# A hybrid attention layer on one core: how stacks, values and bias tables come in from DRAM

## The chip, the core and the metric

The kernel runs on one core of one Trainium2 chip. The core has a matrix engine (TensorE, PE in the profile, with PEld for its weight loads), three engines for elementwise work (VectorE: DVE, ScalarE: ACT, GpSimd: POOL), a fifth engine that mostly issues transfers (SyncE: SP), and 16 DMA engines that move data between DRAM and the on-chip memory SBUF. SBUF has 128 partitions; matmul results land in a smaller memory, PSUM. Each engine works through its own list of instructions in order. The metric is the device time of one execution in microseconds (us): the median of several executions.

## The reference, cut to what matters

One encoder layer over 1024 tokens (a grid of 16 rows of 64) of width 1024, all in float32: a half-step feed-forward block (FFN1), a mixing block with 16 attention heads of width 64, and a second half-step feed-forward block (FFN2).

```python
x = x + 0.5 * rmsnorm(swiglu(rmsnorm(x, g0), w_gate, w_up, w_down), g1)      # FFN1
q, k, v = split(rmsnorm(x, g2) @ w_qkv)                                      # 16 heads each
o_na  = neighbourhood_attention(q[:, :8], k[:, :8], v[:, :8], rel_bias)      # heads 0..7
o_dil = dilated_mixture_attention(q[:, 8:], k[:, 8:], v[:, 8:], t5_bias)     # heads 8..15
x = x + rmsnorm(concat(rmsnorm(o_na, ga), rmsnorm(o_dil, gb)) @ w_out, g3)
x = x + 0.5 * rmsnorm(swiglu(rmsnorm(x, g4), w_gate2, w_up2, w_down2), g5)   # FFN2
```

In neighbourhood attention a query at (row, column) of the grid sees 8 rows by 16 columns of keys around it, with a learned bias by row and column distance. The dilated mixture computes, for every head, sliding windows over each token's neighbours with dilations 1, 4 and 16 (window 128, 512, 2048), with a bias by distance, and merges the three by their softmax denominators.

## The kernel before, in words

**Stages.** FFN1 comes first; the first matmul of the values starts at 683.7 us, the first scores at 941.0, and the last scores at 1194.6 ; pieces of the output projection run between the last heads, and the rest of it and FFN2 follow. The large matrix products use seven block products in place of eight, each as three matmuls of float32 operands split into a rounded upper part and the remainder (`hi`, `lo`).

**q and k.** The projection makes q and k of two heads (a pair p, 128 columns) at a time, in the order of `QK_ORDER`: pairs 4 to 7 (dilated) first, then 0 to 3 (neighbourhood). `QKPairs.put` splits each into upper part and remainder, which lie in the tile `e` of [128 partitions, 2, 512 tokens], and POOL writes them to a DRAM tile `c.qk[p][kind]` of shape [2, 128, 1024]: upper parts first, then remainders. In three cases the tokens are reordered on the way: q of the neighbourhood pairs (`strip`) comes by strips of 8 grid columns, k of the dilated pairs by token number modulo 4.

**Stacks.** A head's scores take two accumulating matmuls over 128 partitions: the 64 rows of q's upper part above the 64 rows of its remainder, against k's upper part (written into both halves), then against k's remainder (both halves). So `load_stack` fills a tile `st` of [128, 3, 1024]: slot 0 is q (upper part in partitions 0 to 63, remainder in 64 to 127), slots 1 and 2 are k's upper part and remainder, the same in both halves. It issues four transfers on POOL, two for each half of 64 partitions.

**Heads.** Attention goes through 16 heads, the eight dilated ones first (heads 0 to 7 in what follows) and the eight neighbourhood ones behind them (8 to 15). Each head is cut into units, and `Ctx.unit` runs them as a pipeline: scores on PE, bias and row maximum on DVE (`maxes`), exponentials on ACT (`exps`), transposes on PE (`turn`), copies back on ACT or DVE (`copy`), the product with the values on PE (`outs`). A dilated head has two parts of four units: `part` 1 for the dilations 4 and 16 with values `vb`, `part` 0 for dilation 1 with values `va`. For part 1, POOL first makes a copy `q` of slot 0 sorted by token number modulo 4 (`q_by_residue`). A neighbourhood head has eight units, one for each strip. Its bias table is `nb`, of which POOL adds the column mask `cmask` into a second half.

**What is loaded ahead.** `load_head` asks for a head's stack (POOL queue), for the values if the head is the first of its pair (SP queue), and then for its bias table (SP queue). `next_head` keeps one or two heads asked for ahead. In the dilated part, every third head's stack and bias table go to a pool of their own (`c.op`), so there are three stack buffers; in the neighbourhood part there are two (`c.stk`), so the stack of head n+2 waits until the scores of head n are done.

**Values in DRAM.** All values of a group of heads lie in `c.v[g]`, [1024 tokens, 4 pairs x 130], in the order of the tokens (a head has 64 columns and one of ones). `vrows` and `vearly` write them on POOL, 128 tokens at a time. `dil_values` reads them for the windows of dilation 1 (`va`: 11 blocks of 128 keys, each block sorted by token number modulo 4) in 12 transfers over 32 partitions, and for dilation 4 (`vb`) in 4 over 128; it is called twice, for the first pair and then for the other three together. `na_v` reads a pair's values by strips, `vs`, in 16 transfers of 8 partitions each.

**Order.** PE, DVE and ACT run in the order in which the program is written (`manual_schedule`). POOL and SP instructions are placed by a scheduler, by what each waits for; on the chip each of these two works through its list in order, so an instruction that waits holds up those behind it, the issuing of transfers included.

Of the kernel before, what the change touches and what calls it, by code (L numbers as in the profile page):

```python
# [19 lines left out]
P, T = 128, 512  # L20
# [776 lines left out]
class QKPairs:  # L797
# [19 lines left out]
    def put(self, b, kind, h, x):  # L817
# [18 lines left out]
        d = c.qk[p][kind]  # L836
        for j in range(2):
            if strip:
                dst = d[j].rearrange("p (s r c) -> p s (r c)", s=8, r=16)[:, :, h * 64:h * 64 + 64]
                nc.gpsimd.dma_start(dst, e[:, j].bitcast(F32).rearrange("p (s x) -> p s x", s=8))  # L840
            elif kind and p >= NP:
                dst = d[j].rearrange("p (c h t) -> p h c t", c=4, h=2)[:, h]
                nc.gpsimd.dma_start(dst, parts[j].bitcast(F32))
            else:
                nc.gpsimd.dma_start(d[j, :, h * T:(h + 1) * T], e[:, j].bitcast(F32))


def load_stack(c, p, hd, pool):

    nc = c.nc  # L850
    st = pool.tile([P, 3, SEQ], F32R, tag="st", name="st", bufs=2 if pool is c.stk else 1)
    rows = slice(hd * 64, hd * 64 + 64)
    q, k = c.qk[p]
    for u in range(2):
        dst = slice(u * 64, u * 64 + 64)
        nc.gpsimd.dma_start(st[dst, 0, :], q[u, rows, :])
        nc.gpsimd.dma_start(st[dst, 1:3, :], k[:, rows, :].rearrange("j p n -> p j n"))
    return st
# [41 lines left out]
def dil_values(c, pool, p, n):  # L900

    w, row = n * VW, 16 * VW
    va = pool.tile([P, 11, w], F32, tag="va", name="va", bufs=1)
    vb = pool.tile([P, 4, 2, w], F32, tag="vb", name="vb", bufs=1)
    v = c.v[1][:, (p - NP) * VW:(p - NP) * VW + w]
    for ci in range(4):
        to = va[ci * 32:ci * 32 + 32]
        for u0, m, t0 in ((0, 7, 16), (7, 2, 0), (9, 2, 192)):
            c.nc.sync.dma_start(to[:, u0:u0 + m], bass.AP(tensor=v.tensor, offset=v.offset + ci * 4 * VW + t0 * row,
                                                          ap=[[row, 32], [32 * row, m], [1, w]]))  # L910
    for ci in range(4):
        c.nc.sync.dma_start(vb[:, ci], v.rearrange("(j i c) f -> c i j f", j=2, c=4)[ci])
    return va, vb


class DilPair:
# [17 lines left out]

    def bias(self, hd, third):
        c, nc = self.c, self.c.nc
        g = (c.op if third else c.gp).tile([P, 3, 384], F32, tag="g", name="g", bufs=1 if third else 2)
        for i in range(2):
            nc.sync.dma_start(g[:, 2 - i], c.gab[i][2 * self.pi + hd, :, 127:511])
        return g  # L940
# [10 lines left out]
    def unit(self, hd, st, q, g, part, quad, un, po):  # L951
# [5 lines left out]
        def scores():  # L957
# [4 lines left out]
            for j in range(2):  # L962
# [8 lines left out]
                else:  # L971
# [5 lines left out]
                    ex = sj.rearrange("p (c u t) -> p u c t", c=4, u=2)  # L977
                    pj = pb[:, j].rearrange("p (u c t) -> p u c t", u=2, c=4)
# [79 lines left out]
def na_v(c, p):  # L1058
    vs = c.vp.tile([P, 8, VW], F32, tag="v" + "ab"[p % 2], name="vs")
    src = c.v[0][:, p * VW:(p + 1) * VW].rearrange("(r s c) f -> r c s f", r=16, s=8)  # L1060
    for r in range(16):
        c.nc.sync.dma_start(vs[r * 8:r * 8 + 8], src[r])
    return vs

# [106 lines left out]
def layer(tc, a, out):  # L1171
    nc = tc.nc
    c = Ctx(tc)
    with ExitStack() as ctx:
# [20 lines left out]
        c.qk = [[c.dr.tile([2, P, SEQ], F32, name=f"qk{p}_{k}") for k in range(2)] for p in range(8)]  # L1195
# [138 lines left out]
        def load_head():  # L1334
# [4 lines left out]
            st = load_stack(c, p, hd, c.op if third else c.stk)  # L1339
            if hd == 0:  # L1340
                pairs[p] = DilPair(c, p, attended if p == 2 * NP - 1 else lambda: None) if p >= NP else na_v(c, p)
            loaded.append((pairs[p], st, pairs[p].bias(hd, third) if p >= NP else na_bias(c, p, hd)))
# [15 lines left out]
        with ExitStack() as order:  # L1358
# [64 lines left out]
            def vearly(p, t, ps):  # L1423
# [3 lines left out]
                nc.gpsimd.dma_start(vs1[t] if p == 0 else c.v[0][t * P:(t + 1) * P, :], v)  # L1427
# [18 lines left out]
            def vrows(t, h):  # L1446
                for g in range(t < 4, 2):
                    nc.gpsimd.dma_start(c.v[g][t * P:(t + 1) * P, :], h[:, g])
# [227 lines left out]
```

## Time and profile before

| | |
|---|---|
| median of 3 runs | 1955.64 us (1953.23 to 1959.21) |
| profiled execution: its own time | 1954.08 us |
| its span, first to last instruction | 1952.3 us |
| PE busy | 1867.3 us (96%) |
| DVE, ACT, POOL busy | 1313.9 us (67%), 804.1 us (41%), 325.4 us (17%) |
| mean granted PE clock | 0.980 |
| moved by DMA | 400.97 MB, mean 205 GB/s |
| attention stage | 941 to 1197 us of the span, from the first scores to the end of the last head |

The profiled execution is one of its own; all busy times, waits and durations below come from it, and its own time is compared with its span and with the median of the runs. PE is counted busy from a matmul's start to its modelled end. The granted clock tells at what share of full speed the throttle let PE run in a stretch. A row of a timeline gives the start in us from the start of the span, the duration, the engine, the line of the kernel, the operation and its tiles (out<-in), how many like it follow one another, and in square brackets how long the engine stood idle before it and what ended that. A row of the table of stretches gives, for a window of time, each engine's busy time and instructions, the granted clock, the mean busy share of the 16 DMA engines (1.00 is all of them; it can read a little more), and the rate. POOL's transfers go by the queue q0, SP's by q1.

### The profile page before, as it was taken

How to read it: one execution, taken by the hardware profiler on the slowest of the kernel's cores; microseconds unless marked ns; L12 is line 12 of the kernel's file. 1: busy time of each engine (PE TensorE's matmuls, PEld its weight loads, DVE VectorE, ACT ScalarE, POOL GpSimd, SP SyncE). 2: the span in 40 equal slices, each digit the busy share in tenths (PEclk: the TensorE clock that was granted, in tenths of full speed). 3: DMA queues.
4: the chain of work that ended last, by engine and by line, in shares of the span. 5: the costliest groups of instructions: out<-in, count | busy, mean ns of one | idle time of the engine just before them, and what ended most of it. 6: DMA issues, size and time to landing. Idle time of an engine off the chain costs nothing.

```text
span 1952.3 us, 25216 instructions
## 1 busy us (share of the span) xinstructions
PE 1867.3 (96%) x9044; PEld 1559.5 (80%) x9044; DVE 1313.9 (67%) x2205; ACT 804.1 (41%) x1287; POOL 325.4 (17%) x536
## 2 busy tenths in 40 slices
PE   5999999999999989999899889998999999999997
PEld 4788888888888868778799887776888888888886
DVE  5778776765656766567456556676788777754557
ACT  4522333333534445233567655454222333344332
POOL 2101111111000123233443310121011111110000
PEclk8999999999999999999899989998999999999999
DMA  6555565546976667768997961574556665476663
GB/s 241 214 172 178 178 236 194 211 161 237 324 250 207 244 216 251 242 217 228 281 205 135 199 125 44 183 276 160 168 183 208 233 216 194 153 265 225 197 231 131
DMA packets 165246, 400.97 MB, mean 205 GB/s; under 512 B 18737, under 2 KB 35297, under 8 KB 165121
## 3 DMA queue, kind: packets, MB, share of 16 engines
q1 hardware_dynamic: 113616, 224.63, 36.4%
q0 software_dynamic: 50640, 172.64, 27.8%
q10 hardware_dynamic: 864, 2.10, 0.3%
q8 instruction: 71, 1.16, 0.2%
q14 instruction: 55, 0.44, 0.1%
HBM read 274.84 MB, written 129.50 MB: 207 GB/s over the span
## 4 chain that ended last, share of the span: by engine, by line
PE 78%; DMA 9%; DVE 6%; issue 5%; ACT 1%; POOL 1%; SPq 0%; DVEq 0%; POOLq 0%; ACTq 0%
PE mmp L264 16%; PE mmp L262 16%; PE mmp L263 16%; PE accp L263 7%; PE accp L264 7%; PE accp L262 7%; PE po L993 2%; PE ptp L892 2%; PE trp L170 1%; PE sp L981 1%; DMA vs<-v 1%; PE po L1106 1%; DMA g<-gab 1%; DMA x<-x 1%; DMA va<-v 1%
## 5 line engine op out<-in xcount | busy, mean ns | idle before, releaser
L262 PE MATMUL mmp<-x,whi 128*128 128x512 f32 (+1 forms) x1464 | 579.7, 396 | 7.6 <-ACT whi L355 3.6
L264 PE MATMUL mmp<-x,wlo 128*128 128x512 f32 (+1 forms) x1464 | 574.9, 393 | 1.0 <-DVE wlo L356 1.0
L263 PE MATMUL mmp<-x,whi 128*128 128x512 f32 (+1 forms) x1464 | 574.5, 392 | 0.6 <-DVE x L172 0.5
L262 PEld LDWEIGHTS mmp<-x,whi 128*128 128x128 f32 x1464 | 277.9, 190 | 67.5 <-ACT whi L355 4.2
L264 PEld LDWEIGHTS mmp<-x,wlo 128*128 128x128 f32 x1464 | 277.8, 190 | 62.2 <-DVE wlo L356 1.9
L263 PEld LDWEIGHTS mmp<-x,whi 128*128 128x128 f32 x1464 | 278.1, 190 | 59.8 <-DVE x L172 1.5
L613 DVE TENSOR_TENSOR pw<-praw,pw 128x1024 fp32r<-128x1024 f32 (+1 forms) x182 | 199.3, 1138 | 122.8 <-ACT pw L612 122.4
L612 ACT CAST pw<-praw 128x1024 fp32r<-128x1024 f32 (+1 forms) x182 | 169.5, 983 | 206.0 <-PE accp L264 167.7
L355 ACT CAST whi<-wraw 128x1024 fp32r<-128x1024 f32 x129 | 135.2, 1050 | 249.4 <-PE mmp L263 216.7
L262 PE MATMUL accp<-pw 128*128 128x512 f32 x600 | 234.4, 391 | 0.6 <-DVE hb L684 0.6
L264 PE MATMUL accp<-pw 128*128 128x512 f32 x600 | 233.5, 389 | 0.0
L263 PE MATMUL accp<-pw 128*128 128x512 f32 x600 | 233.4, 389 | 0.0
L356 DVE TENSOR_TENSOR wlo<-wraw,whi 128x1024 fp32r<-128x1024 f32 x129 | 157.6, 1225 | 24.9 <-ACT whi L355 24.8
L262 PEld LDWEIGHTS accp<-pw 128*128 128x128 f32 x600 | 112.6, 188 | 24.2 <-issue 1.0
L264 PEld LDWEIGHTS accp<-pw 128*128 128x128 f32 x600 | 112.6, 188 | 23.5
L263 PEld LDWEIGHTS accp<-pw 128*128 128x128 f32 x600 | 112.7, 188 | 23.3
L560 POOL DMA_DIRECT2D g<-sg x44 | 23.9, 542 | 472.3 <-DVE sg L553 285.6
L374 ACT COPY s<-mmp 128x512 f32<-128x512 f32 x52 | 30.5, 587 | 147.9 <-PE mmp L264 146.3
L518 DVE TENSOR_TENSOR c<-mmp,u 128x512 f32<-128x512 f32 x52 | 35.9, 691 | 82.5 <-PE mmp L264 82.2
L172 DVE TENSOR_TENSOR x<-trp,x 128x512 fp32r<-128x512 f32 x84 | 57.2, 687 | 35.0 <-ACT x L171 35.0
L355 ACT CAST whi<-traw 128x512 fp32r<-128x512 f32 x52 | 32.3, 621 | 116.9 <-PE mmp L263 58.4
L443 DVE TENSOR_TENSOR wraw<-wraw 128x1024 f32<-128x1024 f32 x52 | 63.6, 1224 | 23.6 <-DMA wraw<-in_wqk_dram 12.5
(230 smaller groups left out, 2739.2 us busy)
## 6 DMA issues: line engine op xcount, KB each, us to landing
praw<-g SPq DMA_DIRECT2D x70, 512.0 KB
wraw<-in_wg_dram SPq DMA_DIRECT2D x44, 512.0 KB
wraw<-in_wu_dram SPq DMA_DIRECT2D x44, 512.0 KB
tr<-in_wd_dram SPq DMA_DIRECT2D x44, 512.0 KB
g<-sg POOLq DMA_DIRECT2D x88, 256.0 KB, 3.9
ts<-tr POOLq DMA_DIRECT2D x22, 1024.0 KB, 4.7
praw<-ts SPq DMA_DIRECT2D x88, 256.0 KB
praw<-in_wd_dram SPq DMA_DIRECT2D x66, 256.0 KB
```

What stands on the lines that cost most here:

```text
L172: nc.vector.tensor_sub(lo, ps, hi.bitcast(F32))
L262: nc.tensor.matmul(out, ahi, bhi, start=start, stop=False, skip_group_check=go_on)
L263: nc.tensor.matmul(out, ahi, blo, start=False, stop=False, skip_group_check=go_on)
L264: nc.tensor.matmul(out, alo, bhi, start=False, stop=stop, skip_group_check=go_on)
L355: nc.scalar.copy(hi, raw)
L356: nc.vector.tensor_sub(lo, raw, hi.bitcast(F32))
L443: nc.vector.tensor_sub(r[:, 0:2], r[:, 1:3], r[:, 0:2])
L518: nc.vector.tensor_add(c21, d, u2)
L612: nc.scalar.copy(w[side][:, 0, :m], raw[:, :m])
L613: nc.vector.tensor_sub(w[side][:, 1, :m], raw[:, :m], w[side][:, 0, :m].bitcast(F32))
L892: c.nc.tensor.transpose(self.tps[:, j, :], self.probs[:, j * P:(j + 1) * P], c.ident)
L993: nc.tensor.matmul(po[0][:, un * 2 + j], u.pt[:, 2 * j + t, :], rhs, start=t == 0, stop=t == 1)
```

## The change: layouts in DRAM, and the order of asking

Four things are changed; the arithmetic stays as it is.

1. **Stacks.** `c.qk` has the shape [128, 2, 1024]: a row's upper part and remainder lie behind each other. `load_stack` issues two transfers of 128 partitions where there were four of 64. Their source patterns are written out as lists of [step, count], outermost first: for q [1024, 2], [2048, 64], [1, 1024]; for k [0, 2], [2048, 64], [1, 2048], where the step of 0 reads the same 64 rows twice. The writes of `put` that don't reorder tokens (48 before) become one transfer each instead of two.
2. **Values in the order of their use.** Rows of `c.v[0]` are ordered by strip, grid row and column in the strip, and those of `c.v[1]` in blocks of 64 tokens by the token number modulo 4. `put_values` writes 128 tokens as two transfers of 64 partitions, where there was one. `dil_values` has 3 transfers over 128 partitions for `va` in place of 12 over 32, and 8 of one block for `vb` in place of 4 of two blocks; `na_v` has 1 in place of 16.
3. **Bias ahead of values.** `load_head` asks for a head's bias table before a pair's values (`DilPair.bias` becomes the function `dil_bias`).
4. **Exponentials of part 0.** Since `va` now holds each block of 128 keys as two half blocks sorted by token number modulo 4, the exponentials read and write in groups of 16 (`m c i`) where they did so in groups of 32 (`u c t`). Their number and size stay.

```diff
@@ QKPairs.put
         d = c.qk[p][kind]
+        if not strip and not (kind and p >= NP):
+            nc.gpsimd.dma_start(d[:, :, h * T:(h + 1) * T], e.bitcast(F32))
+            return
         for j in range(2):
             if strip:
-                dst = d[j].rearrange("p (s r c) -> p s (r c)", s=8, r=16)[:, :, h * 64:h * 64 + 64]
+                dst = d[:, j].rearrange("p (s r c) -> p s (r c)", s=8, r=16)[:, :, h * 64:h * 64 + 64]
...
-            else:
-                nc.gpsimd.dma_start(d[j, :, h * T:(h + 1) * T], e[:, j].bitcast(F32))
@@ load_stack
     st = pool.tile([P, 3, SEQ], F32R, tag="st", name="st", bufs=2 if pool is c.stk else 1)
-    rows = slice(hd * 64, hd * 64 + 64)
-    q, k = c.qk[p]
-    for u in range(2):
-        dst = slice(u * 64, u * 64 + 64)
-        nc.gpsimd.dma_start(st[dst, 0, :], q[u, rows, :])
-        nc.gpsimd.dma_start(st[dst, 1:3, :], k[:, rows, :].rearrange("j p n -> p j n"))
+    q, k = [bass.AP(tensor=x.tensor, offset=x.offset + hd * 64 * 2 * SEQ, ap=[[step, 2], [2 * SEQ, 64], [1, n]])
+            for x, step, n in zip(c.qk[p], (SEQ, 0), (SEQ, 2 * SEQ))]
+    nc.gpsimd.dma_start(st[:, 0, :], q)
+    nc.gpsimd.dma_start(st[:, 1:3, :].rearrange("p j n -> p (j n)"), k)
     return st
@@ dil_values
-    w, row = n * VW, 16 * VW
+    w, row = n * VW, 64 * 4 * VW
...
-    for ci in range(4):
-        to = va[ci * 32:ci * 32 + 32]
-        for u0, m, t0 in ((0, 7, 16), (7, 2, 0), (9, 2, 192)):
-            c.nc.sync.dma_start(to[:, u0:u0 + m], bass.AP(tensor=v.tensor, offset=v.offset + ci * 4 * VW + t0 * row,
-                                                          ap=[[row, 32], [32 * row, m], [1, w]]))
-    for ci in range(4):
-        c.nc.sync.dma_start(vb[:, ci], v.rearrange("(j i c) f -> c i j f", j=2, c=4)[ci])
+    v, at = c.v[1], c.v[1].offset + (p - NP) * VW
+    for u0, m, m0 in ((0, 7, 1), (7, 2, 0), (9, 2, 12)):
+        c.nc.sync.dma_start(va[:, u0:u0 + m], bass.AP(tensor=v.tensor, offset=at + m0 * row,
+                                                      ap=[[4 * VW, P], [2 * row, m], [1, w]]))
+    for ci in range(4):
+        for j in range(2):
+            c.nc.sync.dma_start(vb[:, ci, j], bass.AP(tensor=v.tensor, offset=at + 8 * j * row + ci * 16 * 4 * VW,
+                                                      ap=[[row, 8], [4 * VW, 16], [1, w]]))
     return va, vb
+
+
+def dil_bias(c, pi, hd, third):
+    g = (c.op if third else c.gp).tile([P, 3, 384], F32, tag="g", name="g", bufs=1 if third else 2)
+    for i in range(2):
+        c.nc.sync.dma_start(g[:, 2 - i], c.gab[i][2 * pi + hd, :, 127:511])
+    return g
@@ DilPair.unit
-                    ex = sj.rearrange("p (c u t) -> p u c t", c=4, u=2)
-                    pj = pb[:, j].rearrange("p (u c t) -> p u c t", u=2, c=4)
+                    ex = sj.rearrange("p (c m i) -> p m c i", c=4, m=4)
+                    pj = pb[:, j].rearrange("p (m c i) -> p m c i", m=4, c=4)
@@ na_v
-    src = c.v[0][:, p * VW:(p + 1) * VW].rearrange("(r s c) f -> r c s f", r=16, s=8)
-    for r in range(16):
-        c.nc.sync.dma_start(vs[r * 8:r * 8 + 8], src[r])
+    c.nc.sync.dma_start(vs, c.v[0][:, p * VW:(p + 1) * VW].rearrange("(s p) f -> p s f", s=8))
     return vs
+
+
+def put_values(c, g, t, x):
+
+    for i in range(2):
+        if g:
+            dst = c.v[1].rearrange("(m c i) f -> m i c f", c=4, i=16)[2 * t + i]
+        else:
+            dst = c.v[0].rearrange("(s r c) f -> r s c f", s=8, r=16)[2 * t + i]
+        c.nc.gpsimd.dma_start(dst, x[i * 64:i * 64 + 64])
@@ the DRAM tiles
-        c.qk = [[c.dr.tile([2, P, SEQ], F32, name=f"qk{p}_{k}") for k in range(2)] for p in range(8)]
+        c.qk = [[c.dr.tile([P, 2, SEQ], F32, name=f"qk{p}_{k}") for k in range(2)] for p in range(8)]
@@ load_head
             st = load_stack(c, p, hd, c.op if third else c.stk)
+            g = dil_bias(c, p - NP, hd, third) if p >= NP else na_bias(c, p, hd)
             if hd == 0:
                 pairs[p] = DilPair(c, p, attended if p == 2 * NP - 1 else lambda: None) if p >= NP else na_v(c, p)
-            loaded.append((pairs[p], st, pairs[p].bias(hd, third) if p >= NP else na_bias(c, p, hd)))
+            loaded.append((pairs[p], st, g))
```

In `vearly` and `vrows`, where a write to `c.v[g]` stood, `put_values` is called.

The scheduler's order of SP changes where the first dilated heads are asked for, at the end of the q and k projections. `va` and `vb` are the two value tiles of dilated pairs (those ending in 130 of the first pair, in 390 of the three others), `g` is a head's bias table, `v1` and `gab` are their DRAM tiles; "x2" means two alike in a row. Before:

```order
L909 DMA va_7186<-v1_88 32x2x130 x2
L912 DMA vb_7187<-v1_88 128x2x130 x4
L939 DMA g_7204<-gab0_68 128x384
L939 DMA g_7204<-gab1_69 128x384
L939 DMA g_7414<-gab0_68 128x384
L939 DMA g_7414<-gab1_69 128x384
L909 DMA va_7493<-v1_88 32x7x390
L909 DMA va_7493<-v1_88 32x2x390 x2
```

And now, the same place of SP:

```order
L918 DMA g_7189<-gab0_68 128x384
L918 DMA g_7189<-gab1_69 128x384
L906 DMA va_7192<-v1_88 128x7x130
L906 DMA va_7192<-v1_88 128x2x130 x2
L910 DMA vb_7193<-v1_88 128x1x130 x8
L918 DMA g_7406<-gab0_68 128x384
L918 DMA g_7406<-gab1_69 128x384
L918 DMA g_7482<-gab0_68 128x384
L918 DMA g_7482<-gab1_69 128x384
L906 DMA va_7485<-v1_88 128x7x390
L906 DMA va_7485<-v1_88 128x2x390 x2
```

The bias of head 0 stands ahead of the first pair's values, and the bias tables of head 1 and of head 2 (the first of the second pair) ahead of the values of the three other pairs.

On POOL, among the neighbourhood heads, `st` is a stack, `qk` its two DRAM tiles (`_0` for q, `_1` for k), and the TENSOR_TENSOR adds the column mask into a bias table. Before:

```order
L1537 TENSOR_TENSOR nb_9072<-nb_9072,cmask_7481 128x384
L856 DMA st_9230<-qk1_0_73 64x1024
L857 DMA st_9230<-qk1_1_74 64x2x1024
L856 DMA st_9230<-qk1_0_73 64x1024
L857 DMA st_9230<-qk1_1_74 64x2x1024
L1537 TENSOR_TENSOR nb_9252<-nb_9252,cmask_7481 128x384
```

And now:

```order
L1548 TENSOR_TENSOR nb_9027<-nb_9027,cmask_7472 128x384
L855 DMA st_9185<-qk1_0_73 128x1x1024
L856 DMA st_9185<-qk1_1_74 128x1x2048
L1548 TENSOR_TENSOR nb_9188<-nb_9188,cmask_7472 128x384
L855 DMA st_9331<-qk1_0_73 128x1x1024
L856 DMA st_9331<-qk1_1_74 128x1x2048
```

A stack's two transfers stand where its four stood, each of 128 rows. The orders of PE, DVE and ACT are the same before and now, apart from line numbers.

More of the change, by code (lines that the diff above doesn't have):

```diff
@@ L836, in put @@
         d = c.qk[p][kind]
+        if not strip and not (kind and p >= NP):
+            nc.gpsimd.dma_start(d[:, :, h * T:(h + 1) * T], e.bitcast(F32))
+            return
         for j in range(2):
             if strip:
-                dst = d[j].rearrange("p (s r c) -> p s (r c)", s=8, r=16)[:, :, h * 64:h * 64 + 64]
+                dst = d[:, j].rearrange("p (s r c) -> p s (r c)", s=8, r=16)[:, :, h * 64:h * 64 + 64]
                 nc.gpsimd.dma_start(dst, e[:, j].bitcast(F32).rearrange("p (s x) -> p s x", s=8))
-            elif kind and p >= NP:
-                dst = d[j].rearrange("p (c h t) -> p h c t", c=4, h=2)[:, h]
+            else:
+                dst = d[:, j].rearrange("p (c h t) -> p h c t", c=4, h=2)[:, h]
                 nc.gpsimd.dma_start(dst, parts[j].bitcast(F32))
-            else:
-                nc.gpsimd.dma_start(d[j, :, h * T:(h + 1) * T], e[:, j].bitcast(F32))
 def load_stack(c, p, hd, pool):
@@ L933, in outputs @@
         self.ob = c.op.tile([P, 8, RW], F32, tag="ob", name="ob")
[L935 to L940, printed above, removed]
     def head(self, hd, st, q, g, late, parts=(1, 0)):
@@ L1059, in na_v @@
     vs = c.vp.tile([P, 8, VW], F32, tag="v" + "ab"[p % 2], name="vs")
[L1060 to L1063 removed]
+    c.nc.sync.dma_start(vs, c.v[0][:, p * VW:(p + 1) * VW].rearrange("(s p) f -> p s f", s=8))
+    return vs
+def put_values(c, g, t, x):
+    for i in range(2):
+        if g:
+            dst = c.v[1].rearrange("(m c i) f -> m i c f", c=4, i=16)[2 * t + i]
+        else:
+            dst = c.v[0].rearrange("(s r c) f -> r s c f", s=8, r=16)[2 * t + i]
+        c.nc.gpsimd.dma_start(dst, x[i * 64:i * 64 + 64])
 def na_bias(c, p, hd):
@@ L1426, in vearly @@
                 nc.scalar.copy(by_head(v), ps.rearrange("p (h f) -> p h f", f=64))
-                nc.gpsimd.dma_start(vs1[t] if p == 0 else c.v[0][t * P:(t + 1) * P, :], v)
+                if p == 0:
+                    nc.gpsimd.dma_start(vs1[t], v)
+                else:
+                    put_values(c, 0, t, v)
             vp = Passes(c, 4, op, getv, vearly)
@@ L1447, in vrows @@
                 for g in range(t < 4, 2):
-                    nc.gpsimd.dma_start(c.v[g][t * P:(t + 1) * P, :], h[:, g])
+                    put_values(c, g, t, h[:, g])
             vp.take = combine(c, lambda t, g, h: None, vrows, True)
```

1 line of the change is left out of this document (removed).

## The prediction, as it was made before the run

> **What bounds the kernel now.** I read the page first (span, busy shares), then a table of stretches over the attention stage, then the timelines of PE and POOL there, and last the transfers from issue to landing.
>
> ```profile
> span 1952.3 us, 25216 instructions
> PE 1867.3 (96%) x9044; PEld 1559.5 (80%) x9044; DVE 1313.9 (67%) x2205; ACT 804.1 (41%) x1287; POOL 325.4 (17%) x536
> ...
> core 0: us, PE busy (x) PEld busy (x) DVE busy (x) ACT busy (x) POOL busy (x), PEclk, DMA share, GB/s
> 980.00:997.00 17.00, 12.88 (x92) 12.65 (x90) 7.92 (x35) 8.72 (x20) 7.66 (x8) 0.80 1.04 218
> 997.00:1070.00 73.00, 72.64 (x644) 72.40 (x642) 49.11 (x208) 54.06 (x124) 27.75 (x30) 1.00 0.79 153
> 1070.00:1114.00 44.00, 42.49 (x346) 40.93 (x344) 29.98 (x116) 31.28 (x70) 19.83 (x25) 1.00 1.12 199
> 1114.00:1143.00 29.00, 18.14 (x87) 16.81 (x86) 11.68 (x29) 11.37 (x26) 4.72 (x7) 0.59 0.64 117
> ```
>
> PE is busy for 96% of the span, so a change in transfers can only matter where PE stands still. Everything the change touches is used in the attention stage (941 to 1197 us). Dilated heads 0 to 7 run until 1070; from 997 to 1070 PE is full at full clock. Neighbourhood heads 8 to 15 follow, and there PE waits and then runs at a clock of 0.59. The waits, and the POOL instructions that issue the stacks:
>
> ```profile
> 984.70 1.97 PE L993 MATMUL po<-va,pt 128*128 128x65 f32 x8 [4.12 <-ACT pt L897]
> 988.27 1.81 PE L993 MATMUL po<-va,pt 128*128 128x65 f32 x8
> 991.03 1.00 PE L993 MATMUL po<-vb,pt 128*128 128x65 f32 x8
> ...
> 1070.17 0.49 PE L1093 MATMUL sp<-st 128*128 128x256 f32 x2
> 1092.24 0.48 PE L1093 MATMUL sp<-st 128*128 128x256 f32 x2 [0.20 <-DMA st<-qk]
> 1103.77 0.48 PE L1093 MATMUL sp<-st 128*128 128x256 f32 x2 [1.21 <-DMA st<-qk]
> 1120.03 0.77 PE L1093 MATMUL sp<-st 128*128 128x256 f32 x2 [5.96 <-DMA st<-qk]
> 1131.25 1.54 PE L1106 MATMUL po<-vs,pt 128*128 128x65 f32 x6 [4.90 <-ACT pt L897]
> 1160.09 0.49 PE L1093 MATMUL sp<-st 128*128 128x256 f32 x2
> ...
> 1055.14 0.57 POOL L856 DMA_DIRECT2D st<-qk  x1 [9.47 <-issue]
> 1081.19 0.57 POOL L856 DMA_DIRECT2D st<-qk  x1 [4.57 <-PE sp L1093]
> 1101.71 0.57 POOL L856 DMA_DIRECT2D st<-qk  x1 [1.58 <-PE sp L1093]
> 1142.33 0.55 POOL L856 DMA_DIRECT2D st<-qk  x1 [10.08 <-PE sp L1093]
> ```
>
> The PE rows are the first scores of heads 8 (1070), 10, 11, 12 and 14 (1160); the POOL rows start the stacks of heads 8, 10, 12 and 14. In the neighbourhood heads a stack waits for the buffer of the head before last ("<-PE sp L1093"), so it has one head's time to land: head 10's is asked for at 1081.19 and needed at 1092.04. It lands 0.20 us late. So this stretch is already set by the landing of stacks; there is no slack. The other two waits are late tables:
>
> ```profile
> 961.24 21.02 DMA g<-gab
> 1104.69 15.58 DMA vs<-v
> 1120.35 9.34 DMA nb<-nb
> ```
>
> These pieces of the chain of waits end at 982.26 (a dilated bias queued on SP behind values; PE stands 4.12 us) and at 1129.7 (a neighbourhood bias behind value pieces; 4.90 us).
>
> **The change part by part.** *Stacks.* Four transfers of 64 rows become two, and each now has an outermost dimension of 2 in DRAM: [2, 64, 1024] for q, [2 with step 0, 64, 2048] for k. How such a transfer is dealt out to the 16 DMA engines decides everything. The trace has one POOL pair with a small outermost dimension, the dilated tables at L784 to L785, whose pattern has 8 outermost:
>
> ```profile
> ts<-tr POOLq DMA_DIRECT2D x22, 1024.0 KB, 4.7
> gab<-tab POOLq DMA_DIRECT2D x2, 2044.0 KB, 19.2
> L785 POOL DMA_DIRECT2D gab<-tab x2: 1072/1088/1104, 806.5 to 807.6; - x2
> DMA to landing us min/median/max: 18.2/19.2/20.2
> ...
> 809.00:812.00 3.00, 2.71 (x12) 2.25 (x13) 2.57 (x4) 0.00 (x0) 3.00 (x6) 1.00 0.59 215
> 812.00:822.00 10.00, 10.00 (x46) 8.28 (x45) 3.57 (x5) 1.05 (x1) 0.04 (x1) 1.00 1.03 258
> ```
>
> Two tables of 2 MB, issued 1.1 us apart on one queue, both take about 19 us, where a transfer of 1 MB over 128 rows takes 4.7. Had each used all 16 engines in turn, the first would have landed in about half the time of the second. Early on the engines are 0.59 busy, later 1.03. I read this as: a transfer with 8 outermost runs on 8 engines, the next one on other 8. With 2 outermost, q and k would run on 2 engines each.
>
> The Trainium skill (DMA: Bandwidth & Descriptors, "Rules for kernel authors") speaks against this change in so many words: an outermost dimension smaller than 16, such as a leading zero-stride broadcast, confines the whole transfer to that many engines. The two tables agree with it; no run so far shows a case of two.
>
> Then the landing. Each of k's two engines carries 64 rows of 8 KB, 512 KB. An estimate of an engine's rate from both sides: the 1 MB transfer puts 64 KB on each engine in 4.7 us, of which about 2 us are fixed (the quickest small table below), so 2.7 us per 64 KB: 8 x 2.7 + 2.0 = 23.6 us. All of POOL's queue moved 172.64 MB in 27.8% of 16 x 1952.3 us, 19.9 GB/s per engine: 26.4 + 2.0 = 28.4 us. With nothing taken off, 8 x 4.7 = 37.6 us is the far end. I take 26 us for k; q has half, about 14.
>
> ```profile
> DMA to landing us min/median/max: 2.0/3.5/19.3
> q0 software_dynamic: 50640, 172.64, 27.8%
> ```
>
> (The first row is of the neighbourhood table nb.) The skill's page gives ~27 GiB/s per engine (its "Specifications"); by that, an estimate, k would land in about 20 us and the sum below come out near 1968.
>
> Each stall is the landing less the time there was between issue and need. Head 8: 1070.17 - 1055.14 = 15.0, stall 11.0. Head 10: 10.9, stall 15.1. Head 12: needed at 1120.03 - 5.96 = 1114.07, 12.4, stall 13.6. Head 14: 17.8, stall 8.2. Heads 9, 11, 13 and 15 gain what the head before them lost (head 9: some 12 + 14 = 26 us) and don't wait. In the dilated heads only head 1 is short:
>
> ```profile
> 941.36 0.55 POOL L856 DMA_DIRECT2D st<-qk  x1
> 961.34 0.75 PE L981 MATMUL sp<-st,q 128*128 128x256 f32 x4 [0.43 <-POOL q L863]
> 997.26 0.73 PE L981 MATMUL sp<-st,q 128*128 128x256 f32 x4
> 1011.73 0.71 PE L981 MATMUL sp<-st,q 128*128 128x256 f32 x4
> 995.24 2.06 POOL L863 CAST q<-st 128x1024 fp32r<-128x1024 f32 x1 [7.51 <-DMA st<-qk]
> ```
>
> 19.5 us there against 26: 6.5. The later ones have three buffers, so two heads of 14.5 us (997.26 to 1011.73) as cover: 28.9 against 26, 0. That cover is thin: POOL copies q in order between the stacks (the row at 995.24), so a stack follows the last by q's landing and some 4 us, 18 against 14.5; at worst 4 heads x 3.5 = 14 us. After each stall PE runs at half clock: the eight matmuls take 1.97 and 1.81 us until 990 and then 1.00, so about 3 us are lost, five times. Together 54.4 + 15 = 69.4.
>
> *Bias ahead of values, values in the order of use.* SP issues 6 + 16 transfers of dilated values for 24 + 8, one per pair of neighbourhood heads for 16, and each bias stands ahead of its pair's values. What this takes away: 4.12 and some 2.5 of half clock at 984; in the second half 0.20 + 1.21 + 5.96 + 4.90 = 12.3, and about 8 of the 18.14 busy us at clock 0.59. Together 27. The vb pieces have 8 outermost, so 8 engines; 1.6 MB at 19.9 GB/s each is 10 us, asked for around 945 and used after 985, nothing.
>
> *Writes.* POOL issues 32 value writes for 16, and 48 of q and k for 64, at 0.55 to 0.92 us each: it comes out even, and PE matmuls of the projections hide it (without that cover, some 9 us). The orders of PE, DVE and ACT stay as they are. The exponentials' regrouping is the same count over a shorter run:
>
> ```profile
> L886 ACT ACTIVATE s<-s,ob 128x256 f32<-128x256 f32 x64 | 29.0, 504 | 9.5 <-DVE ob L881 9.5
> L886 ACT ACTIVATE pb<-s,sa 128x256 f32<-128x256 f32 x64 | 28.9, 503 | 3.3 <-DVE sa L881 3.0
> ```
>
> Regrouped ones cost 503 ns, plain ones 504: 0. A tenth more would be 3 us on ACT, beside PE.
>
> Sum: 69.4 - 27 = 42 us. The profiled execution took 1954.08 us, 1.78 above its span; 1954 + 42 = 1996, and as it lies 1.6 us under the median of the runs shown, I forecast **1998 us**.
>
> **The rivals.** *It goes the other way: 16 engines.* If the 128 partitions of the destination decide, a stack has 1.5 MB over 16 engines: 2.0 + 1.5 x 2.7 = 6 us. For it: 64-row transfers are slow now, so there is something to win:
>
> ```profile
> st<-qk POOLq DMA_DIRECT2D x32, 512.0 KB, 10.5
> ```
>
> Half of what ts moves takes twice as long. Against it: the two tables. It decides below 10.9 us, head 10's time; then all 27 us go: 1956 - 27 = 1929. *Two engines and slower rows.* At 37.6 us the five stalls grow by 58, and the dilated heads lose the cover: 2055 to 2070. For it: in the crowded stretches engines are over 1.0 busy; against it, q0's mean rate has those stretches in it. *It cancels.* The landing at which 69 shrinks to 27 is 26 - 42 / 5 = 17.5 us; for that an engine would have to move 34 GB/s, and no row shows it: about 1956. Forecast and first rival differ in whether the change does what its words say: the transfers reach 128 partitions either way, but not by 16 engines.
>
> **How the numbers follow.** The forecast has 0.74, the faster rival 0.11, the slower rows 0.12, the cancelling 0.03. Five stalls move by 5 us for each us of landing: 23.6 gives 1986, 28.4 gives 2010, which is the likeliest case's own range, and with the thin cover in the dilated heads up to 2024. Out to 2045 it takes in half of the slow rows; down to 1968 the stalls that overlap better than I count. That leaves out the faster rival and the far end: 1968 to 2045. A measurement of this kernel tells 0.3% (6 us) from no change: faster 0.11, same 0.03, slower 0.86.
>
> **What would show it.** Right: the 32 stack transfers land at some 14 us (q) and 26 us (k), PE's longest waits are first scores of heads 8, 10, 12 and 14 for stacks, 8 to 15 us each, and the clock from 1070 on is far under 1; the waits of 4.12 and 4.90 for biases are gone. Wrong: landings under 11 us and a neighbourhood part without waits (16 engines), or dilated heads that wait for the copy of q (the cover was too thin), or waits of the values' pieces on 8 engines.

## The result, and the profile after

The changed kernel takes 2067.83 us (median of 4 runs, 2058.80 to 2075.85), the kernel before 1957.12 (4 runs, 1953.23 to 1959.21). The ratio is 1.0567, 95% interval 1.0512 to 1.0622. Slower, as forecast, but by 111 us instead of 42. The profiled execution took 2058.80 us, 104.7 more than that of before. Where one execution stood far outside its set (2339 us in one experiment below, where the others took about 1942), it is left out of the figures.

The page of the changed kernel (span, engines, packets, and POOL's queue), and behind it the row of packets before:

```profile
span 2057.0 us, 25041 instructions
PE 1872.8 (91%) x9044; PEld 1565.6 (76%) x9044; DVE 1312.4 (64%) x2205; ACT 803.4 (39%) x1287; POOL 316.9 (15%) x504
...
DMA packets 191132, 401.07 MB, mean 195 GB/s; under 512 B 46672, under 2 KB 63232, under 8 KB 188960
...
q0 software_dynamic: 77264, 172.75, 24.3%
```

```profile
DMA packets 165246, 400.97 MB, mean 205 GB/s; under 512 B 18737, under 2 KB 35297, under 8 KB 165121
```

PE does the same 9044 matmuls in 5.5 us more of busy time, so nearly all of the loss is PE standing still. The bytes are the same but for 0.1 MB, but POOL's queue has 26624 more packets (77264 against 50640), and the packets under 512 B have grown from 18737 to 46672. (Of the 64 writes of q and k before, 32, and not 48, leave the tokens in their order; these became 16.)

The issues of the changed kernel, with KB of each and us to landing:

```profile
st<-qk POOLq DMA_DIRECT2D x16, 1024.0 KB, 27.7
...
st<-qk POOLq DMA_DIRECT2D x16, 512.0 KB, 16.6
```

k lands in 27.7 us and q in 16.6, where 26 and 14 were forecast. The timeline of the changed kernel (ACT, PE and POOL), cut to the longest waits:

```profile
917.54 1.85 POOL L843 DMA_DIRECT2D qk<-qk  x2 [2.02 <-ACT qk L834]
919.38 0.70 POOL L838 DMA_DIRECT2D qk<-qk  x1
...
948.94 0.63 ACT L829 ACTIVATE qk<-c 128x512 f32<-128x512 f32 x1 [19.71 <-DMA qk<-qk]
...
953.31 0.76 PE L262 MATMUL mmp<-x,whi 128*128 128x512 f32 x1 [19.50 <-DVE v L489]
...
998.51 1.19 PE L980 MATMUL sp<-st,q 128*128 128x256 f32 x4 [22.52 <-DMA st<-qk]
...
1050.72 1.97 PE L992 MATMUL po<-vb,pt 128*128 128x65 f32 x8 [8.73 <-ACT pt L896]
...
1072.64 1.97 PE L992 MATMUL po<-vb,pt 128*128 128x65 f32 x8 [6.89 <-ACT pt L896]
...
1139.76 0.77 PE L1100 MATMUL sp<-st 128*128 128x256 f32 x2 [13.79 <-DMA st<-qk]
1155.43 0.48 PE L1100 MATMUL sp<-st 128*128 128x256 f32 x2 [2.05 <-DMA st<-qk]
...
1182.02 0.80 PE L1100 MATMUL sp<-st 128*128 128x256 f32 x2 [16.47 <-DMA st<-qk]
...
1222.90 0.76 PE L1100 MATMUL sp<-st 128*128 128x256 f32 x2 [17.68 <-DMA st<-qk]
...
1265.03 0.80 PE L1100 MATMUL sp<-st 128*128 128x256 f32 x2 [9.51 <-DMA st<-qk]
```

The last five rows are the first scores of heads 8, 9, 10, 12 and 14. Rows 998, 1050 and 1072 are heads 1, 3 and 4. Row 953 is before any head: the last products of the q and k projection wait 19.50 us, because ACT (948.94) waits for a tile whose write POOL had issued at 917 to 919.

The chain of waits of the changed kernel, four pieces of it (start, us, what):

```profile
919.38 31.21 DMA qk<-qk
...
961.44 36.94 DMA st<-qk
...
1016.70 12.23 DMA ob<-ob
1028.95 19.48 DMA obn<-ob
```

The first is that write, issued right behind the stack of head 0. The third and fourth are on SP's queue: the regrouping of a dilated pair's outputs through DRAM.

Because PE's order is the same in both kernels, each matmul can be compared with itself. How much later the first score of a head comes than in the profile before (us; "proj." is a matmul of the projections at 840 us):

```
            proj.   h0    h1    h2    h3    h4    h5    h8    h9   h10   h12   h13   h14   end
changed     -1.6  19.2  37.2  39.7  32.7  43.8  54.0  69.6  73.5  89.8 102.9  95.2 104.9 104.8
```

The gain that was forecast can be seen in two places (h2 to h3, -7.0; h12 to h13, -7.7): the waits for late bias tables are gone. The rest are losses.

### The profile page after: what moved, and what is told of

Same layout as the page of the kernel before. It is cut to its first block, busy times and chain, and to the rows that moved or that the text cites. A ratio compares the mean times of both kernels' runs of the same rounds, so it can differ in the third digit from the quotient of the medians.

```text
span 2057.0 us, 25041 instructions
## 1 busy us (share of the span) xinstructions
PE 1872.8 (91%) x9044; PEld 1565.6 (76%) x9044; DVE 1312.4 (64%) x2205; ACT 803.4 (39%) x1287; POOL 316.9 (15%) x504
## 2 busy tenths in 40 slices
DMA packets 191132, 401.07 MB, mean 195 GB/s; under 512 B 46672, under 2 KB 63232, under 8 KB 188960
## 3 DMA queue, kind: packets, MB, share of 16 engines
q0 software_dynamic: 77264, 172.75, 24.3%
## 4 chain that ended last, share of the span: by engine, by line
PE 73%; DMA 15%; DVE 5%; issue 5%; POOL 2%; ACT 1%; SPq 0%; DVEq 0%; POOLq 0%; ACTq 0%
PE mmp L264 14%; PE mmp L262 14%; PE mmp L263 14%; DMA st<-qk 9%; PE accp L263 8%; PE accp L262 8%; PE accp L264 8%; DMA qk<-qk 2%; PE trp L170 1%; PE po L1113 1%; PE ptp L891 1%; PE po L992 1%; DMA obn<-ob 1%; PE sp L1100 1%; DMA x<-x 1%
## 5 line engine op out<-in xcount | busy, mean ns | idle before, releaser
L262 PE MATMUL mmp<-x,whi 128*128 128x512 f32 (+1 forms) x1464 | 580.6, 397 | 27.1 <-DVE v L489 19.5
L262 PEld LDWEIGHTS mmp<-x,whi 128*128 128x128 f32 x1464 | 278.5, 190 | 87.2 <-issue 19.9
L355 ACT CAST whi<-wraw 128x1024 fp32r<-128x1024 f32 x129 | 135.2, 1050 | 252.4 <-PE mmp L263 218.8
L896 ACT COPY pt<-ptp 128x512 f32<-128x512 f32 (+2 forms) x96 | 49.7, 519 | 123.8 <-PE ptp L891 123.3
L1100 PE MATMUL sp<-st 128*128 128x384 f32 (+1 forms) x128 | 39.6, 393 | 59.5 <-DMA st<-qk 59.5
```

Of the source, the lines that this page charges most:

```text
L262: nc.tensor.matmul(out, ahi, bhi, start=start, stop=False, skip_group_check=go_on)
L355: nc.scalar.copy(hi, raw)
L896: (c.nc.vector.tensor_copy if self.count % 4 == 3 else c.nc.scalar.copy)(self.pt[:, :self.n], self.tps[:, :self.n])
L1100: nc.tensor.matmul(pv, st[:, 0, s * P:(s + 1) * P], keys, start=i == 0, stop=i == 1)
```

## The experiments

Two theories stood at the start. *Engines*: a stack's outermost dimension of 2 confines it to two DMA engines. *Layout*: the new value pieces, or two large transfers of 128 partitions, are at fault. In each diff, lines of the one kernel are - and those of the experiment +.

### The two outer dimensions swapped (against the changed kernel)

```diff
-    q, k = [bass.AP(tensor=x.tensor, offset=x.offset + hd * 64 * 2 * SEQ, ap=[[step, 2], [2 * SEQ, 64], [1, n]])
+    q, k = [bass.AP(tensor=x.tensor, offset=x.offset + hd * 64 * 2 * SEQ, ap=[[2 * SEQ, 64], [step, 2], [1, n]])
```

> The changed kernel with one edit: in both source patterns of a stack the two outer dimensions are swapped, [[2 SEQ, 64], [SEQ or 0, 2], [1, n]] for [[SEQ or 0, 2], [2 SEQ, 64], [1, n]], so partition 2r holds row r's first copy and 2r+1 its second. Same two transfers, same 128 partitions, same bytes and packets; a score sums over partitions, so their order does not matter. Theory (a transfer runs on as many DMA engines as its outermost dimension in DRAM has steps, here 2): now 64 steps outermost, so all 16 engines; k lands in 5 to 8 us where it took 27.7, no first score of a head waits over 1 us, the writes of the projections no longer stand 30 us behind a stack, and the time is about 1930 us (the time before less the 27 us that the prediction gave to the bias and value waits), 1920 to 1945. Rival (two transfers of 128 partitions, or the new value layout and its pieces, cause the stalls): landing and time stay, 2055 to 2075.

Measured: 1924.34 us, ratio to the kernel before 0.9854 (0.9835 to 0.9872). A row of its page, and its issues of stacks:

```profile
DMA packets 162460, 400.96 MB, mean 209 GB/s; under 512 B 18000, under 2 KB 34560, under 8 KB 160288
```

```profile
st<-qk POOLq DMA_DIRECT2D x16, 1024.0 KB, 7.3
...
st<-qk POOLq DMA_DIRECT2D x16, 512.0 KB, 4.8
```

One swap is worth 143 us. Transfers, bytes and partitions are the same; k lands in 7.3 us for 27.7, and no first score of a head waits. The small packets tell how many engines worked: 46672 - 18000 = 28672 fewer (of 4 bytes each in the trace's records of packets), which is 32 transfers x 14 x 64. That fits fourteen engines which got 64 empty packets each, for the 64 real packets that each of the two others carried. The records name no engine, but their times agree: of the 128 packets of 8 KB that bring head 0's k, mostly two and never more than three are in flight at once in the changed kernel, over 27.8 us, and up to 17 in the swapped one, over 5.5 us (records that follow one another overlap a little). So two engines are a reading that both counts bear out; that the outermost dimension decides is shown.

### Four transfers of 64 rows (against the changed kernel)

```diff
-    q, k = [bass.AP(tensor=x.tensor, offset=x.offset + hd * 64 * 2 * SEQ, ap=[[step, 2], [2 * SEQ, 64], [1, n]])
-            for x, step, n in zip(c.qk[p], (SEQ, 0), (SEQ, 2 * SEQ))]
-    nc.gpsimd.dma_start(st[:, 0, :], q)
-    nc.gpsimd.dma_start(st[:, 1:3, :].rearrange("p j n -> p (j n)"), k)
+    rows = slice(hd * 64, hd * 64 + 64)
+    q, k = c.qk[p]
+    for u in range(2):
+        dst = slice(u * 64, u * 64 + 64)
+        nc.gpsimd.dma_start(st[dst, 0, :], q[rows, u, :])
+        nc.gpsimd.dma_start(st[dst, 1:3, :], k[rows])
```

> The changed kernel, its layouts and its order of asking, but each stack in four transfers of 64 rows as before. Theory (engines): 64 rows outermost, so 16 engines; landing at most the 10.5 us of the kernel before (k's rows are now 8 KB in one piece where they were two of 4 KB), time 1928 to 1945, some us behind the interleaved one at most, since POOL issues 32 transfers more. Rival (the values' new layout and pieces are at fault): over 1960. Second rival (what counts is the number of transfers, not the engines): the interleaved kernel beats this one by over 6 us.

Measured: 1942.75 us, ratio 0.9947 (0.9932 to 0.9962). 64 rows outermost are enough to undo the loss, but the kernel is 18 us behind the swapped one, as the second rival had it. Its issues and a wait of PE:

```profile
st<-qk POOLq DMA_DIRECT2D x32, 512.0 KB, 9.4
...
st<-qk POOLq DMA_DIRECT2D x32, 256.0 KB, 7.6
```

```profile
1008.37 1.87 PE L994 MATMUL po<-vb,pt 128*128 128x65 f32 x8 [3.63 <-ACT pt L898]
```

Each transfer has half the bytes and takes longer. In the trace's records of packets, an 8 KB packet of a stack takes 696 ns here (median, 985 to 1090 us) and 325 in the swapped kernel. The next experiment asks whether the number of transfers does that, or where they write.

### Even and odd partitions (against the four transfers of 64 rows)

```diff
-        dst = slice(u * 64, u * 64 + 64)
-        nc.gpsimd.dma_start(st[dst, 0, :], q[rows, u, :])
-        nc.gpsimd.dma_start(st[dst, 1:3, :], k[rows])
+        nc.gpsimd.dma_start(st[u::2, 0, :], q[rows, u, :])
+        nc.gpsimd.dma_start(st[u::2, 1:3, :], k[rows])
```

> The four-transfer kernel of the first series with one edit: the two copies of a row go to the even and to the odd partitions instead of to partitions 0 to 63 and 64 to 127. Same four transfers of 64 rows, same bytes, packets and source rows outermost. In the four-transfer kernel an 8 KB packet of a stack took 660 ns, in the interleaved one 325. Theory (a transfer that writes into only one half of the partitions has half the rate): spread over all 128 partitions the packets take about 325 ns again, and the time is that of the interleaved kernel plus a little for 32 more issues: 1924 to 1931. Rival (it is the number of transfers, or the 64 rows each, that costs): packets stay at about 650 ns and the time at 1940 to 1945.

Measured: 1922.42 us, ratio 0.9841 (0.9818 to 0.9863). Its issues:

```profile
st<-qk POOLq DMA_DIRECT2D x32, 512.0 KB, 6.8
...
st<-qk POOLq DMA_DIRECT2D x32, 256.0 KB, 5.5
```

Still four transfers of 64 rows, but an 8 KB packet takes 325 ns again, and the loss of 18 us is gone. It is the half of the partitions that costs, not the number of transfers. The Trainium skill (SBUF — State Buffer, "Door 1: The DMA port swizzle") says that the partitions which a transfer reaches decide how many of 16 ports it uses, that partitions 0 to 63 reach half of them, and that 64 in a row are thus little better than 32. The packets, 696 ns against 325, agree.

### The stack part alone, in the kernel before

```diff
-    rows = slice(hd * 64, hd * 64 + 64)
-    q, k = c.qk[p]
-    for u in range(2):
...
+    q, k = [bass.AP(tensor=x.tensor, offset=x.offset + hd * 64 * 2 * SEQ, ap=[[step, 2], [2 * SEQ, 64], [1, n]])
+            for x, step, n in zip(c.qk[p], (SEQ, 0), (SEQ, 2 * SEQ))]
+    nc.gpsimd.dma_start(st[:, 0, :], q)
+    nc.gpsimd.dma_start(st[:, 1:3, :].rearrange("p j n -> p (j n)"), k)
...
-        c.qk = [[c.dr.tile([2, P, SEQ], F32, name=f"qk{p}_{k}") for k in range(2)] for p in range(8)]
+        c.qk = [[c.dr.tile([P, 2, SEQ], F32, name=f"qk{p}_{k}") for k in range(2)] for p in range(8)]
```

The writes of `put` follow the new shape, as in the changed kernel; values and bias tables stay as before.

> The kernel before with the stack part of the change alone (layout of q and k, two transfers a stack with 2 outermost); values and bias tables as before. Theory (engines): landings of 16 and 27 us as in the changed kernel, the same stalls at heads 0, 1, 8, 10, 12 and 14, and the two late bias tables on top as far as they don't hide behind those: 2065 to 2095. Rival (the long waits of the changed kernel come from the new value pieces sharing engines with the stacks): the stall of 19.5 us before the first head is gone and the time is under 2050.

Measured: 2072.56 us, ratio 1.0616 (1.0594 to 1.0638). PE waits before head 0 and in head 1 here too, with the old value pieces:

```profile
957.98 0.77 PE L262 MATMUL mmp<-x,whi 128*128 128x512 f32 x1 [18.20 <-DVE v L489]
...
1009.65 1.19 PE L980 MATMUL sp<-st,q 128*128 128x256 f32 x4 [28.21 <-DMA st<-qk]
```

So the stacks are the whole loss; the new value layout is not needed for it.

### The first pair's stacks swapped, the others as changed

```diff
-    q, k = [bass.AP(tensor=x.tensor, offset=x.offset + hd * 64 * 2 * SEQ, ap=[[step, 2], [2 * SEQ, 64], [1, n]])
+    first = p == QK_ORDER[0]
+    q, k = [bass.AP(tensor=x.tensor, offset=x.offset + hd * 64 * 2 * SEQ,
+                    ap=([[2 * SEQ, 64], [step, 2]] if first else [[step, 2], [2 * SEQ, 64]]) + [[1, n]])
```

> The changed kernel, but the stacks of heads 0 and 1 (the first pair) with the two outer dimensions swapped, the other 14 as changed. Theory (engines, and whatever stands behind a stack on POOL's queue lands with it): the writes of the projections behind head 0's stack land in 6 to 8 us instead of 30, the 19.5 us of PE before head 0 and most of the 22.5 us before head 1 are gone: 36 to 41 us under the changed kernel, 2020 to 2035. Rival (the 19.5 us come from the bias of head 1, which POOL awaited for 23.7 us and which stands behind value pieces on SP's queue): only head 1's wait goes, 2042 to 2052.

Measured: 2038.85 us, ratio 1.0437 (1.0417 to 1.0457): 29 us under the changed kernel, less than expected. The issues of this kernel between 922 and 926 us, and PE's wait in head 2:

```profile
qk<-qk POOLq DMA_DIRECT2D x2, 256.0 KB, 7.1
qk<-qk POOLq DMA_DIRECT2D x1, 512.0 KB, 7.7
```

```profile
997.44 1.19 PE L982 MATMUL sp<-st,q 128*128 128x256 f32 x4 [21.53 <-DMA st<-qk]
```

The same writes behind head 0's stack land in 7.1 and 7.7 us, where they took 30.2 to 31.2 (the chain's first piece), and the 19.50 us are gone. So a stack of two engines holds up what is queued behind it. It holds up the other queue too, as POOL's wait for head 1's bias table tells, in the changed kernel and in this one:

```profile
943.79 0.85 POOL L862 COPY g<-g 128x384 f32<-128x384 f32 x1 [23.70 <-DMA g<-gab]
...
935.28 0.89 POOL L864 COPY g<-g 128x384 f32<-128x384 f32 x1 [8.70 <-DMA g<-gab]
```

The table comes by SP's queue, which carries no stack and issues the same transfers in the same order in both kernels; what the two queues share are the DMA engines. So 15 of the 23.70 us come with the slow stack, and not from the value pieces ahead of the table. PE does not stand for the 8.70 that are left, and the rival is out. Whether POOL's longer wait would have held PE up by itself was not separated; the chain of the changed kernel names the writes. The gain was smaller because head 2, whose stack is the first slow one here, now waits 21.53 us: the loss went from head 1 to head 2.

### Only the neighbourhood heads' stacks on two engines

```diff
-    q, k = [bass.AP(tensor=x.tensor, offset=x.offset + hd * 64 * 2 * SEQ, ap=[[step, 2], [2 * SEQ, 64], [1, n]])
+    swap = p >= NP
+    q, k = [bass.AP(tensor=x.tensor, offset=x.offset + hd * 64 * 2 * SEQ,
+                    ap=([[2 * SEQ, 64], [step, 2]] if swap else [[step, 2], [2 * SEQ, 64]]) + [[1, n]])
```

> The changed kernel with the two outer dimensions swapped for the dilated heads' stacks (8 heads), the neighbourhood heads' stacks as changed (2 outermost). Theory (the prediction's four neighbourhood stalls were sized about right; what it lacked lies in the dilated heads): the dilated heads run as in the interleaved kernel, heads 8, 10, 12 and 14 wait 10 to 18 us each, 55 to 60 in all, with 8 to 15 us of low clock: 1924 + 65 to 75, so 1988 to 2000. Rival (the neighbourhood stalls were made long by what the late dilated heads left behind): waits of 48 us or less in all and a time under 1980.

Measured: 1998.16 us, ratio 1.0235 (1.0207 to 1.0263). PE's waits of this kernel in heads 8, 10, 12 and 14:

```profile
1070.70 0.76 PE L1102 MATMUL sp<-st 128*128 128x256 f32 x2 [13.37 <-DMA st<-qk]
...
1118.52 0.80 PE L1102 MATMUL sp<-st 128*128 128x256 f32 x2 [18.84 <-DMA st<-qk]
...
1160.53 0.77 PE L1102 MATMUL sp<-st 128*128 128x256 f32 x2 [17.65 <-DMA st<-qk]
...
1201.22 0.80 PE L1102 MATMUL sp<-st 128*128 128x256 f32 x2 [9.04 <-DMA st<-qk]
```

58.9 us in four waits, which is what the changed kernel has in the same places (57.5). They are the neighbourhood heads' own; the late dilated heads leave them nothing. The other 70 us between this kernel and the changed one belong to the stacks of the dilated heads.

### The good stacks alone, in the kernel before

The diff is against the kernel of the stack part alone.

```diff
-    q, k = [bass.AP(tensor=x.tensor, offset=x.offset + hd * 64 * 2 * SEQ, ap=[[step, 2], [2 * SEQ, 64], [1, n]])
+    q, k = [bass.AP(tensor=x.tensor, offset=x.offset + hd * 64 * 2 * SEQ, ap=[[2 * SEQ, 64], [step, 2], [1, n]])
```

> The kernel before with the stack part alone, in the good order of dimensions (row outermost, its two copies behind each other): 16 engines and all 128 partitions; values and bias tables as before. Theory (parts add up: stacks' waits of 0.20, 1.21 and 5.96 us and some low clock go, the two late bias tables with 4.12 and 4.90 us stay): 10 to 16 us under the kernel before, 1937 to 1944. Rival (the slow stacks were what made the bias tables late): 25 us or more under it, as in the interleaved kernel.

Measured: 1924.76 us, ratio 0.9866 (0.9843 to 0.9889). The rival was right: fast stacks alone give what all three parts gave together. In its profiled execution one old wait is left, in head 2; the wait of 4.90 us in head 12 is gone though no bias table is asked for earlier.

```profile
982.74 1.97 PE L992 MATMUL po<-va,pt 128*128 128x65 f32 x8 [3.33 <-ACT pt L896]
```

### One line of the kernel before: even and odd partitions

```diff
-        dst = slice(u * 64, u * 64 + 64)
+        dst = slice(u, P, 2)
```

> The kernel before with one line changed: the two copies of a stack's rows go to even and odd partitions, dst = slice(u, 128, 2), where they went to 0 to 63 and 64 to 127. Layout in DRAM, four transfers a stack, 4 KB packets, values and order of asking as before. Theory (all the gain of the good kernels is the stacks' rate, and that is set by how a transfer spreads over engines and over partitions): the 4 KB packets take about 175 ns instead of 358, k lands in 6 to 8 us, and the time is that of the other good kernels within their scatter, 1921 to 1930. Rival (the [128, 2, 1024] layout with its 8 KB rows, or the fewer writes, carries part of the gain): 1935 to 1945.

Measured: 1929.91 us, ratio 0.9875 (0.9854 to 0.9897). Old layout, four transfers, 4 KB packets: such a packet takes 174 ns for 358 before (medians, 985 to 1090 us), k lands in 6.6 us for 10.5, and 23 us are gained. It ends at the slow edge of what the theory gave; whether the layout's 8 KB rows add a few us, the overlapping intervals don't tell.

### Values alone, bias order alone

```diff
             st = load_stack(c, p, hd, c.op if third else c.stk)
+            g = dil_bias(c, p - NP, hd, third) if p >= NP else na_bias(c, p, hd)
             if hd == 0:
...
-            loaded.append((pairs[p], st, pairs[p].bias(hd, third) if p >= NP else na_bias(c, p, hd)))
+            loaded.append((pairs[p], st, g))
```

Shown is the bias order in the kernel before. The kernel with the values alone takes `dil_values`, `na_v`, `put_values` and the exponentials' grouping from the change's diff, word for word, with the calls in `vearly` and `vrows`.

> The kernel before with values in the order of their use alone (their writes, their reads, the exponentials' grouping); stacks as before, and bias tables still asked for behind values. The four-transfer kernel, which has this and the bias order, was 10.6 us under the kernel before. Theory (the value pieces made the neighbourhood bias late): most of that, 6 to 10 us under the kernel before, with the 4.90 us wait before head 13's values gone and the 4.12 us wait in head 2 still there. Rival (the gain is the order of asking, and eight pieces of vb on 8 engines cost as much as they save): within 3 us of the kernel before, or slower.

> The kernel before with only the bias tables asked for ahead of values. Theory (in the kernel before, the two late bias tables are a by-product of stacks at half rate; asking earlier removes the 4.12 us wait of head 2 and its low clock, while the waits for stacks in heads 10 to 12 stay, and the 4.90 us wait stays or moves): 3 to 8 us under the kernel before. The prediction's reading (both bias waits go with their low clock, and part of the 12.3 us): 15 us or more under it. No gain at all would say that the order of asking was covered.

Measured: 1941.73 us (0.9942, 0.9920 to 0.9963; five executions) with the values alone, 1941.18 us (0.9937, 0.9915 to 0.9959) with the bias order alone. Both together, in the four-transfer kernel, which also has the new layout of q and k, gave 1942.75. Each is worth 11 to 12 us by itself, and the two together no more. With the values alone the 4.90 us went as expected, and the 4.12 us went too, but heads 1 and 2 wait 2.71 and 2.86 us for POOL's copy of q there; the 6 to 10 us expected were a little low. With the bias order alone the 4.12 us went, and a wait of 4.38 us, whose cause the trace does not name, stands a few units behind the place of the 4.90. The 3 to 8 us expected were too low, and the prediction's reading (15 or more) too high.

### Each of them with the good stacks

> The kernel before with stacks in the good order of dimensions (16 engines, 128 partitions) and values in the order of their use; bias tables still behind values. With the fast stacks alone the trace kept one wait of the old ones: 3.33 us in head 2 for a bias table, and some 4 us of low clock behind it; with all three parts it was gone. Theory (either of the two other parts removes that wait): no wait over 1 us in head 2, some 7 us less at head 3's first scores than with the stacks alone, 1917 to 1925. Rival (only the order of asking removes it): the wait of 3 us stays, 1924 to 1931.

> The kernel before with stacks in the good order of dimensions and the bias tables asked for ahead of values; values in their old layout. Theory (either of the two parts removes the 3.33 us wait of head 2): gone, 1917 to 1925. Rival (only the values' layout does): the wait stays, 1924 to 1931. Where both kernels end within 2 us of the stacks alone (1924.8), the values and the order of asking are worth nothing that a measurement can tell once the stacks are fast.

Both are the kernel with the good stacks alone, plus one of the two parts. Measured: 1923.44 us (0.9843, 0.9822 to 0.9864) and 1926.07 us (0.9845, 0.9827 to 0.9864). In both profiled executions head 2's wait is gone, so either part removes it; but the medians lie within 2 us of 1924.76, the second one above the 1917 to 1925 that were expected. With fast stacks, values and order are worth nothing that these measurements tell apart.

## Why the prediction was wrong

Its direction and its cause were right, its sum was too small: 2067.83 lies 23 us above the range. By the stretches of the table of heads, forecast against found:

```
                                forecast        found
before head 0                        0           20.8   (-1.6 to 19.2)
heads 1 and 2                  6.5 + 3           20.5   (19.2 to 39.7)
late bias of head 2               -6.6           -7.0   (39.7 to 32.7)
heads 3 to 7, "thin cover"           0           22.9   (32.7 to 55.6)
heads 8 to 15     47.9 + 12 - 20.3 = 39.6        49.2   (55.6 to 104.8)
sum                                 42.5       106.4
```

The 55.6 is the delay of the last matmul ahead of head 8; in the table of heads, h8 has head 8's own wait in it.

**The landing was right.** 27.7 us for 26, 16.6 for 14, from rates of rows that had nothing to do with two engines. It is partly luck: the lower of the two rates, 19.9 GB/s an engine, was the mean of a queue whose own stacks ran at half rate, and a packet of 8 KB took 346 ns in the changed kernel (median, 985 to 1090 us), so that 64 of them alone are 22 us. The rule of the Trainium skill that the prediction weighed (DMA: Bandwidth & Descriptors, "Rules for kernel authors") held; the swap shows it here. The estimate of 20 us for k, from the Trainium skill's rate of an engine, was too low.

**The four neighbourhood stalls were right in place and 9.6 us short in size**: 57.5 us for 47.9. Each wait was 1 to 4 us longer than taken, and head 9, which was not to wait, added 2.05.

**The step that failed is "the time there was between issue and need", applied to the stacks' first users alone.** It costed a slow transfer only by the head that uses it. A transfer that keeps two engines for over 25 us also delays others, on its own queue and on SP's, and these had users of their own:

- *Before head 0* the prediction put nothing. But three of the projections' writes stand behind head 0's stack on POOL's queue; they landed with it, after 30 us, and the tiles that they empty stop ACT, DVE and PE in turn (19.50 us). The sentence on writes counted POOL's time to issue them, not their way through the queue. Swapping the first pair's stacks shows it.
- *Head 1* had 19.5 us of cover on paper. But its stack was asked for right behind a write and 6 us ahead of head 2's stack, with three more writes between them; it was needed 15.3 us after it was asked for, not 19.5, and k landed in 36.9 us instead of 26. Which of the transfers beside it cost how much was not taken apart.
- *Heads 3 and 4* were called thinly covered, at worst 14 us, by POOL's copy of q. What came late was something else: the regrouped outputs on SP's queue (12.23 and 19.48 us in the chain), and a bias table that POOL awaited for 27.18 us. That all of it hangs on the dilated stacks is shown (with those swapped, no such wait is left); that it is through the shared engines is an inference, which head 1's bias table in the experiment with the first pair supports.

**The gain of 27 us was right in size and wrong in cause.** Where stacks are fast, the trace from head 0 on gains 27 to 34 us. But the bias order and the values are not needed for it, and give 11 to 12 us without fast stacks: the stacks of the kernel before were themselves at half rate, each transfer in one half of the partitions, and with fast stacks alone all but 3.33 us of the late tables' waits are gone. That crowding is the way from the one to the other is an inference; the DMA engines were 1.12 busy in the neighbourhood stretch before. The same 44 us of the swapped kernel, which is 11 to 19 us further on in its work there:

```profile
core 0: us, PE busy (x) PEld busy (x) DVE busy (x) ACT busy (x) POOL busy (x), PEclk, DMA share, GB/s
1070.00:1114.00 44.00, 42.20 (x340) 40.45 (x340) 34.46 (x123) 34.88 (x78) 14.06 (x16) 0.99 0.69 227
```

It moves more (227 GB/s for 199) with the engines less busy (0.69 for 1.12). The row "half of what ts moves takes twice as long", which the prediction quoted for its rival, was the clue.

**The rivals.** The faster one was sized right: 1929 for 16 engines, 1924 in the swapped kernel. The slower one (2055 to 2070) has the measured time in it, but by another mechanism: k of heads 8, 10, 12 and 14 landed in 27.5 to 28.4 us, not in 37.6; head 1's, at 36.9, came nearest to it. The pieces of vb on 8 engines and the larger number of value writes show as no wait of PE in the swapped kernel, and a regrouped exponential takes 502 ns in the changed kernel for 503 before: nothing, as said.

## What to carry to other kernels

Write a transfer's pattern in DRAM with a long dimension outermost (64 against 2 here), and let its destination reach over both halves of the partitions; both can be had by ordering rows and copies alone, since a matmul does not care which partition holds which term of its sum. When a transfer gets slower, don't price only its user: list what stands behind it in its queue and what else is in flight while it lands. And when tables are late while the DMA engines are full, first ask what fills them; the cure was in the stacks (28 us), and earlier asking alone gave 12.

## What the runs showed of the hardware

A packet into partitions 0 to 63 or 64 to 127 takes about twice as long as one of a transfer into all 128, or into every second one: 696 against 325 ns for 8 KB, 358 against 174 for 4 KB. A transfer with 2 outermost brings 896 packets of 4 bytes (28672 over 32 transfers) more than the same one with 64 outermost, and mostly two packets of its data are in flight at once, against up to 17. A write of 256 KB behind one landed after 30.2 us, where it takes 7.1. And while such a stack was on its way, a table on SP's queue kept POOL waiting for 23.70 us instead of 8.70.
